# Layer 0's feed-forward down projection with 60 slabs set sooner, four half-depth tiles and eight plain quads, and layer 1's memory keys and values ahead of the keys

## Chip, cores and metric

One core of one Trainium2 chip. The metric is the device time of one execution of the kernel in microseconds (us). Engines: TensorE (PE, the matrix engine; its weight loads are shown apart as PEld), VectorE (DVE), ScalarE (ACT), GpSimd (POOL) and SyncE (SP). SP issues the plain DMAs, POOL those that add while they write.

## What is computed

A two-layer decoder trunk for 256 tokens (T) of width 2048, in float32. Cut to what matters here:

```python
def squared_relu_mlp(h, w1, w2):          # w1 2048x8192, w2 8192x2048
    z = jax.nn.relu(h @ w1)
    return (z * z) @ w2

def reference(x, mem, ...):
    for i in range(2):
        if i == 1:
            sk1, sk2, sv = shared_kv(x, ...)          # rms_norm(x) @ w_kv: keys, then values
        u = rms_norm(x, mix_norm[i]) @ w_in[i]
        ...                                           # i == 0: pooling mixer; i == 1: differential attention
        mem_out = memory_cross_attention(mem_q, mem, mem_norm[i], w_mem_kv[i], ...)
        x = x + concatenate([token_out, mem_out]) @ w_out[i]
        x = x + squared_relu_mlp(rms_norm(x, ffn_norm[i]), w_ff1[i], w_ff2[i])
    return x

def memory_cross_attention(q, mem, mem_norm_g, w_mem_kv, mq_g, mk_g):
    mkv = rms_norm(mem, mem_norm_g) @ w_mem_kv        # its keys and values need only mem, not x
    ...
```

## The kernel before

**Numbers in two parts.** Each float32 operand is split into a high part, rounded to the matrix engine's format, and a low part, the rest. A product is high times high, high times low and low times high, added in PSUM. ScalarE makes the high part (a cast, L177), VectorE the low one (a subtraction, L180).

**Weights.** They lie in memory in the order of use, as blocks of 128 by 128. `Feed` loads them (SP, L141 to L145), splits them and keeps the parts in a ring of six places of 512 columns (`SLOTS`). Four blocks are a quad. `fill` (L226) prepares every quad or slab job three items (`AHEAD`) before its use, and `load` (L125) loads three items more. Plain weights use four raw buffers (`raw`) of 8 blocks.

**A hand-written order.** The program is written as one sequence. `at(d, fn)` puts work `d` ticks later; `tick()` is called once a quad and, where it is written so, once a job. A scheduler at compile time then orders each engine's instructions by this sequence and by its own estimate of when each is ready, so an engine's order may leave the written one.

**Forms of a product.**
- `a_part` (L420): weights stand in the array, 128 outputs wide, and the tokens stream. For a block: one matmul of 512 columns (the high weights by high and low tokens) and one of 256 (the low weights).
- `c_tile` (L443): the same with three matmuls of 256 columns, so that the result needs no addition of two halves.
- `wide_step` (L455): tokens stand in the array, 512 outputs stream; six matmuls of 512 columns for a quad. `b_tile` and `map_tile` run 16 of these over the 16 chunks of the input.

**The feed-forward part, `ffn` (L731), once a layer.** 64 up tiles (`up_tile`, 16 blocks each) make the 64 chunks of z; each goes through a copy (L761), an addition, a ReLU (L824), a square (L832) and a split into z (L772, L776). z holds 16 chunks at a time. The down projection runs between the up tiles by a scheme of seven products in place of eight: a *slab* is two chunks of z (a pair `i`) by 1024 of the 2048 output columns (side `g`: 1 left, 0 right), and its seven products of 128 by 512 go into seven accumulators in PSUM (`banks`). They need sums of z (`combine`, L787, into `sit`, four pairs at a time) and sums of the weights. A slab runs as four jobs (`slab_jobs`, L872) of 6, 3, 6 and 6 matmuls. Its weight sums come from a DMA on POOL's queue that adds to a loaded buffer (`add_right`, L149) and from VectorE's additions (L205, L219). The first job's preparation issues such a DMA for the second, the third one's for the fourth.

There is one set of seven banks for two sides, so every eight slabs a `swap` (L931) copies all banks out and the other side's back. Before, 56 slabs run in each layer: both sides for pairs 0 to 23, then the right side alone for pairs 24 to 31. `tiles_at` (L1034) gives the due time of each slab in up tiles: `p + 8.4` for most, and 1.7 tiles a slab at the end. When the left side ends (pair 23), `close_left` combines its banks, and `turn_left` (L972) transposes it between later up tiles and adds it to the residual.

Twelve jobs are left after up tile 63. `last` (L1097) runs them in pairs between eight `down_tile`s: the left outputs over the remaining chunks 48 to 63 of z, 16 blocks each (`a_part`), with VectorE's additions (L850 to L852). `finish_banks` (L991) closes the right side and transposes it.

**What follows layer 0's feed-forward part.** `done` splits each finished chunk of the residual with its gain into `x_kv`. `later_square` (L710) sums its squares. Then come three key tiles (`map_tile`, 48 quads), three value tiles (48 quads), the memory keys and values of layer 1 (32 quads, input `mems1`), and the queries. `mems1` is made from four reloads of 512 KB of the memory (`mem_again`, L1361), asked for at ticks 46, 55, 64 and 73 into the same four raw buffers as the weights; its 16 chunks are split 6, 8, 10 and 12 ticks after each reload.

## Time and profile before

| | us |
|---|---|
| median of 3 runs | 1997.24 (1997.13 to 1997.51) |
| the profiled execution | 1997.11 |
| its span, first to last instruction | 1995.3 |
| up tiles with slabs, layer 0 | about 268 to 863 |
| the last 12 jobs and 8 down tiles, layer 0 | 863 to 924 |
| key tiles, value tiles | 924 to 991, 991 to 1057 |
| memory keys, memory values | 1057 to 1079, 1079 to 1100 |
| queries and attention, output projection, feed-forward part of layer 1 | 1100 to the end |

How to read the profile: all times are from the start of the span. A row of the timeline is start, duration, engine, line, operation, output and inputs, and count; rows that follow each other closely are merged (`x2`). A duration of a matmul holds its pipelined end, so matmuls overlap, and only the distance between starts tells what one costs. A row of groups is line, engine, operation, output and inputs, shapes and count, then busy time and mean duration in ns, then idle time ahead of them and what ended it. Line numbers are those of the kernel before.

### The profile page before, as it was taken

The numbers are of one execution on the slowest core, as the hardware profiler recorded it, in microseconds if no ns is written. First come the engines' busy times: TensorE is split into PE (matmuls) and PEld (weight loads), VectorE is DVE, ScalarE is ACT, GpSimd is POOL, SyncE is SP. The second block draws the span as 40 slices with busy tenths as digits, with TensorE's granted clock in tenths as the row PEclk, the third lists the DMA queues.
The fourth block names the chain that finished last, engine by engine and source line by source line (L and its number), as shares of the span: only waits on it lengthen the run. The fifth ranks groups of instructions, "written<-read, shape, count | busy, mean of one in ns | idle before, by whom it ended". The sixth has DMA issues, their size and how long they took to land.

```text
span 1995.3 us, 32048 instructions
## 1 busy us (share of the span) xinstructions
PE 1990.6 (100%) x10534; PEld 1704.2 (85%) x10534; DVE 1716.3 (86%) x3089; ACT 1497.9 (75%) x2792; POOL 246.7 (12%) x291
## 2 busy tenths in 40 slices
PE   9999999999999999999999999999999999999999
PEld 8888888888888888888888889888888888888888
DVE  8888878989989899989765698878889898999987
ACT  7765577787887878778665699567787878878775
POOL 0001311111111111110000000311111111111110
PEclk9999999999999999999999999999999999999999
DMA  9556567888888888765566534657888888888775
GB/s 320 174 191 192 189 199 213 225 229 235 227 232 223 226 236 231 220 188 181 189 232 196 172 127 138 200 190 208 228 219 234 230 227 225 227 234 235 218 216 145
DMA packets 142727, 420.10 MB, mean 211 GB/s; under 512 B 16096, under 2 KB 18784, under 8 KB 142560
## 3 DMA queue, kind: packets, MB, share of 16 engines
q1 hardware_dynamic: 110160, 359.32, 55.6%
q0 software_dynamic: 32256, 58.73, 17.4%
q8 instruction: 82, 1.34, 0.3%
q14 instruction: 85, 0.70, 0.1%
q10 hardware_dynamic: 144, 0.01, 0.0%
HBM read 415.90 MB, written 2.10 MB: 209 GB/s over the span
## 4 chain that ended last, share of the span: by engine, by line
PE 100%; DVE 0%; issue 0%
PE x_bank L434 25%; PE x_bank L436 12%; PE p L867 9%; PE p L869 9%; PE p L870 9%; PE wo L434 6%; PE wo L436 3%; PE u L434 2%; PE ff L434 2%; PE u L436 1%; PE q L468 1%; PE k L468 1%; PE q L470 1%; PE q L469 1%; PE k L469 1%; PE v L468 1%
## 5 line engine op out<-in xcount | busy, mean ns | idle before, releaser
L177 ACT CAST hi_ring<-raw 128x512 fp32r<-128x512 f32 x1001 | 613.4, 620 | 270.8 <-PE x_bank L434 69.9
L180 DVE TENSOR_TENSOR lo_ring<-raw,hi_ring 128x512 fp32r<-128x512 f32 x1001 | 687.1, 695 | 121.8 <-ACT hi_ring L177 105.8
L434 PE MATMUL x_bank<-fx,hi_ring 128*128 128x512 f32 x1952 | 610.1, 394 | 0.0
L436 PEld LDWEIGHTS x_bank<-fx,lo_ring 128*128 128x128 f32 x1952 | 366.6, 188 | 83.6
L436 PE MATMUL x_bank<-fx,lo_ring 128*128 128x256 f32 x1952 | 383.5, 278 | 0.0
L434 PEld LDWEIGHTS x_bank<-fx,hi_ring 128*128 128x128 f32 x1952 | 319.8, 189 | 24.1
L177 ACT CAST hi_ring<-room 128x1024 fp32r<-128x1024 f32 x224 | 235.9, 1053 | 128.2 <-PE p L869 107.4
L180 DVE TENSOR_TENSOR lo_ring<-room,hi_ring 128x1024 fp32r<-128x1024 f32 x224 | 274.0, 1223 | 37.6 <-ACT hi_ring L177 29.1
L180 DVE TENSOR_TENSOR lo_ring<-slab,hi_ring 128x512 fp32r<-128x512 f32 (+1 forms) x224 | 213.9, 955 | 60.4 <-ACT hi_ring L177 59.9
L177 ACT CAST hi_ring<-slab 128x512 fp32r<-128x512 f32 (+1 forms) x224 | 185.8, 830 | 40.3 <-PE p L869 23.9
L867 PE MATMUL p<-hi_ring,sit 128*128 128x512 f32 x448 | 175.5, 392 | 0.0
L869 PE MATMUL p<-hi_ring,sit 128*128 128x512 f32 x448 | 175.1, 391 | 0.0
L870 PE MATMUL p<-lo_ring,sit 128*128 128x512 f32 x448 | 174.3, 389 | 0.0
L152 POOL DMA_DIRECT2D room<-in_w x112 | 96.7, 864 | 556.2 <-DVE lo_ring L180 435.3
L152 POOL DMA_DIRECT2D slab<-in_w x112 | 96.9, 865 | 529.1 <-DVE lo_ring L180 513.0
L434 PE MATMUL wo<-cat,hi_ring 128*128 128x512 f32 x512 | 161.7, 397 | 0.0
L867 PE MATMUL p<-hi_ring,z 128*128 128x512 f32 x336 | 132.1, 393 | 0.0
L869 PE MATMUL p<-hi_ring,z 128*128 128x512 f32 x336 | 131.2, 390 | 0.0
L870 PE MATMUL p<-lo_ring,z 128*128 128x512 f32 x336 | 130.8, 389 | 0.0
L436 PEld LDWEIGHTS wo<-cat,lo_ring 128*128 128x128 f32 x512 | 95.9, 188 | 22.3
L436 PE MATMUL wo<-cat,lo_ring 128*128 128x256 f32 x512 | 101.0, 278 | 0.0
L870 PEld LDWEIGHTS p<-lo_ring,sit 128*128 128x128 f32 x448 | 84.1, 188 | 18.6
(373 smaller groups left out, 3372.5 us busy)
## 6 DMA issues: line engine op xcount, KB each, us to landing
raw<-in_w SPq DMA_DIRECT2D x500, 512.0 KB, 4.4
slab<-in_w SPq DMA_DIRECT2D x112, 512.0 KB, 4.7
room<-in_w SPq DMA_DIRECT2D x112, 256.0 KB, 4.7
slab<-in_w POOLq DMA_DIRECT2D x112, 256.0 KB, 6.6
room<-in_w POOLq DMA_DIRECT2D x112, 256.0 KB, 5.8
memraw<-in_mem SPq DMA_DIRECT2D x5, 512.0 KB, 4.4
resid<-in_x SPq DMA_DIRECT2D x8, 256.0 KB, 5.8
out_y<-resid SPq DMA_DIRECT2D x16, 128.0 KB, 1.9
```

The source lines that it names most:

```text
L152: self.nc.gpsimd.dma_start(t, self.wst[h, :, 0:512], accum_op=ALU.add)
L177: self.last_cast = self.nc.scalar.copy(hi, src)
L180: low = self.nc.vector.tensor_sub(lo, src, hi.bitcast(F32))
L434: nc.tensor.matmul(ps, hi, xs[:, k, :], start=first and c == 0, stop=False)
L436: nc.tensor.matmul(ps[:, T : 2 * T], lo, xs[:, k, 0:T], start=False, stop=last and c == len(ks) - 1,)
L468: nc.tensor.matmul(ps[t], x[t][1], hi, start=k == 0, stop=False)
L469: nc.tensor.matmul(ps[t], x[t][0], hi, start=False, stop=False)
L470: nc.tensor.matmul(ps[t], x[t][0], lo, start=False, stop=k == NK - 1)
L867: nc.tensor.matmul(ps, a[1], hi, start=new, stop=False, **again)
L869: nc.tensor.matmul(ps, a[0], hi, start=False, stop=False, **again)
L870: nc.tensor.matmul(ps, a[0], lo, start=False, stop=end, **again)
```

## The change

For layer 0 alone (`full = l == 0`):
- The slabs are 60: after pair 23, the right side for pairs 24 to 27, then the left side for 24 to 27 (with one more swap), then the right side for 28 to 31. The left side closes after pair 27.
- They are due sooner: a new table for the first ones, `p + 7.6` in place of `p + 8.4`, and 0.95 tile a slab at the end. Jobs may all run between the up tiles as far as they are due and their inputs ready.
- `last_full` replaces `last`: all but nine of the jobs left, then half-depth tiles for left outputs 4 to 7 (`c_tile`, chunks 56 to 63 of z only) with three jobs after each of the first three; then eight plain quads (`wide_step`) for left outputs 0 to 3 over the same chunks. The right side is scaled and transposed during these quads, the left side is closed after them (`close`) and transposed during the next stage (`turn_side`). No left transposes run between up tiles.
- `refill` reloads the memory into z's own space during the last jobs, at ticks 1, 5, 10 and 13 after the third half-depth tile, and splits 4 to 7 ticks after each reload.

Then layer 1's memory keys and values run at once, ahead of the key tiles; the squares of the residual are summed during them, and their column form is taken at the key tiles' second tick.

```diff
-    def wide_step(ps, what, xs, k):
+    def wide_step(ps, what, xs, k, ends=(0, NK - 1)):
...
-        slabs += [(0, i, False) for i in range(24, 32)]
+        if full:
+            slabs += [(0, i, True) for i in range(24, 28)]
+            slabs += [(1, i, False) for i in range(24, 28)]
+            slabs += [(1, i, True) for i in range(28, 28)]
+            slabs += [(0, i, False) for i in range(28, 32)]
+        else:
+            slabs += [(0, i, False) for i in range(24, 32)]
+        sooner = (4.5, 6, 8, 9.6, 10.6, 11.5, 12.4, 13.4, 14.4, 15.5, 16.5)
         early = (4.5, 6, 8, 10, 11.2, 12.2, 13.2, 14.2, 15.2, 16.2, 17.4, 18.4)
...
+            if full:
+                if p < 10:
+                    return sooner[p + 1]
+                return p + 7.6 if p <= 50 else 57.6 + 0.95 * (p - 50)
...
-            while len(jobs) > 12:
-                if jobs[0][0] > tiles and (n >= least or not ready(*jobs[0][1:])):
+            while len(jobs) > (0 if full else 12):
+                early_one = jobs[0][0] > tiles
+                if early_one and n >= least or (full or early_one) and not ready(*jobs[0][1:]):
                     break
...
+        def turn_side(side, base, h):
+            t4 = pp.tile([P, 2, T], F32, tag="ot"[h % 2], bufs=1, name="ct")
...
+            c = base + 2 * h
+            nc.vector.tensor_add(resid[:, c : c + 2, :], resid[:, c : c + 2, :], t4)
+            at(1, lambda: done(c))
+            at(2, lambda: done(c + 1))
+
+        def last_full():
+            def some(n):
+                for _ in range(n):
+                    while not ready(*jobs[0][1:]):
+                        tick()
+                    one_job()
+                    tick()
+
+            rest = range(56, 64)
+            some(len(jobs) - 9)
+            for c, t in (("c12", 0), ("v", 1)):
+                scale_rows(left[c], t)
+            for n in range(4, 8):
+                ps = bank()
+                c_tile(ps, "w_ff2", l, n, rest, z)
...
+                at(1, add)
+                if n == 6:
+                    refill(z)
+                if n < 7:
+                    some(3)
+            for d, c, t in ((1, "c11", 0), (2, "c12", 0), (3, "u", 1), (4, "v", 1)):
+                at(d, lambda c=c, t=t: scale_rows(right[c], t))
+            for h in range(4):
+                at((5, 6, 8, 10)[h], lambda h=h: turn_side(right, 8, h))
+            ps = pair_of_banks(0, "ff2")
+            for k in rest:
+                wide_step(ps, ("w_ff2", l, k, 0, 4), z, k % NK, (rest[0] % NK, 63 % NK))
+
+            def close():
+                for t, x in enumerate((left["c11"], left["u"])):
+                    nc.vector.tensor_add(x, x, ps[t])
+                    at(1 + t, lambda x=x, t=t: scale_rows(x, t))
+
+            at(1, close)
+            for e, h in enumerate((2, 3, 0, 1)):
+                at(3 + e, lambda h=h: turn_side(left, 0, h))
...
+    def refill(z):
+        mems_in.append(z)
+
+        def again(p):
+            t = wp.tile([P, 4, T], F32, tag="raw", bufs=RAWS, name="memraw1")
+            nc.sync.dma_start(t, memT[:, 4 * p : 4 * p + 4, :])
+            for k in range(4):
+                at(
+                    4 + k,
+                    lambda k=k: split_gain(z[:, 4 * p + k, :], t[:, k, :], gcol(G_MEM + 16 + 4 * p + k)),
+                )
+
+        for p, d in enumerate((1, 5, 10, 13)):
+            at(d, lambda p=p: again(p))
...
     down()
-    for n in range(NK):
-        at(2 + n // 2, lambda n=n: later_square(n))
+    mems1 = mems_in[0]
+    for i, n in enumerate((8, 9, 10, 11, 12, 13, 14, 15, 0, 1, 2, 3, 4, 5, 6, 7)):
+        at(10 + i, lambda i=i, n=n: later_square(n, i == 0))
+    ps = pair_of_banks(0, "mk1")
+    b_tile(ps, "w_mem_kv", 1, 0, mems1)
+    mrow1 = key_rows(ps, mem_c, P)
+    ps = pair_of_banks(1, "mv1")
+    b_tile(ps, "w_mem_kv", 1, 1, mems1)
...
-    at(12, lambda: c1.extend(columns("x")))
+    at(2, lambda: c1.extend(columns("x")))
     for c in range(3):
         ps = pair_of_banks(c, "k1")
         map_tile(ps, "w_kv", 0, (2 * c, 2 * c + 1, 6 + 2 * c, 7 + 2 * c), x_kv)
```

More of the change, by code (lines that the diff above doesn't have):

```diff
@@ L127, in load @@
             r = self.plan.loads[self.lp]
+            if r[0] == "S" and sum(x[0] == "S" and x[2] == r[2] for x in self.raw) == 3:
+                return
             h = self.plan.row[r]
@@ L960, in close_left @@
                 add(u, u, banks[6])
+            if left is right:
+                return
             for p in of_job[j]:
                 restore(p, 0)
-            if j == 3:
+            if j == 3 and not full:
                 rows = ((left["c11"], 0), (left["c12"], 0), (u, 1), (v, 1))
@@ L1054, in one_job @@
             runs[s](j)
-            if end and s + 1 < len(slabs):
-                if g == 1 and i == 23:
+            if s + 1 == len(slabs):
+                if full:
+                    at(1, lambda: close_left(j, right))
+            elif end:
+                if g == 1 and i == (28 - 1 if full else 23):
                     at(1, lambda: close_left(j))
@@ L1089, in ffn @@
         due(64)
-        assert len(jobs) == 12 and not turns
+        assert full or len(jobs) == 12 and not turns
         feed.loads_ahead = LOADS
```

88 lines of the change are left out of this document (43 added, 45 removed).

## The prediction

> **What bounds the kernel now.** I read the head of the page first, then the chain of waits, then the busy time by stretch, and last the timeline round the end of layer 0's up projection. The columns of the head are busy time, its share of the span, and instructions.
>
> ```profile
> span 1995.3 us, 32048 instructions
> PE 1990.6 (100%) x10534; PEld 1704.2 (85%) x10534; DVE 1716.3 (86%) x3089; ACT 1497.9 (75%) x2792; POOL 246.7 (12%) x291
> PEclk9999999999999999999999999999999999999999
> PE 100%; DVE 0%; issue 0%
> ```
>
> The matrix engine has 4.7 us in which nothing ran, its clock was granted in full throughout, and the chain that ended last stays on it. So an edit pays only through the matrix work it removes, and costs only through a wait that it opens. A busy engine may still be slow, so prices below are taken from start to start, not from the durations, which overlap.
>
> The profiled execution took 1997.11 us, 1.8 us more than its span, and the median of the runs is 1997.24. I sum against 1997.1 and add 0.1 for the median. The next busiest engine decides how much a new wait could cost; here it is by stretch (stretch, its length, then PE, PEld, DVE, ACT, POOL busy with counts, clock, DMA share, GB/s):
>
> ```profile
> 645.00:745.00 100.00, 100.00 (x513) 85.17 (x513) 90.80 (x143) 82.45 (x141) 16.42 (x19) 1.00 0.88 231
> 863.00:924.40 61.40, 61.40 (x340) 53.14 (x339) 57.46 (x105) 46.17 (x84) 3.45 (x4) 1.00 0.60 176
> 924.40:960.00 35.60, 35.60 (x164) 29.59 (x163) 33.47 (x81) 29.44 (x65) 0.00 (x0) 1.00 0.60 187
> 1003.00:1057.00 54.00, 54.00 (x244) 44.81 (x243) 31.55 (x52) 32.50 (x58) 0.00 (x0) 1.00 0.69 229
> 1057.00:1100.00 43.00, 43.00 (x192) 35.59 (x191) 24.34 (x41) 23.11 (x40) 0.00 (x0) 1.00 0.60 192
> 1950.00:1996.00 46.00, 41.61 (x251) 36.74 (x249) 34.02 (x57) 21.88 (x35) 1.73 (x2) 0.99 0.46 136
> ```
>
> Inside the up projection (first row) VectorE is busy for 91%. From the last up tile to the first key step (863 to 924.4) it is 94%, and in the next 36 us 94% again, all without a wait of the matrix engine. The memory keys and values (the row from 1057) load it to 57% only. That is the ground on which the change moves work. (In the last row, 45.3 us to the end of the span, 3.7 us of the idle 4.7 lie behind the last product.)
>
> **The price of a block.** A block is 128 by 128 weights. Four starts give the four prices:
>
> ```profile
> 862.66 0.40 PE L867 MATMUL p<-hi_ring,z 128*128 128x512 f32 x1
> ...
> 864.49 0.39 PE L870 MATMUL p<-lo_ring,sit 128*128 128x512 f32 x1
> ...
> 873.01 0.62 PE L434 MATMUL x_bank<-z,hi_ring 128*128 128x512 f32 x2
> ...
> 877.87 0.63 PE L434 MATMUL x_bank<-z,hi_ring 128*128 128x512 f32 x2
> ```
>
> Eight matmuls of slabs lie between the first two rows: 1.83/8 = 0.229 us each. A slab is 7 products of 3, so 21 x 0.229 = 4.80 us for 16 blocks. Seven pairs of blocks of a down tile lie between the last two: 4.86/7 = 0.694 a pair, 0.347 a block, 5.55 us for 16.
>
> ```profile
> 1985.19 0.28 PE L448 MATMUL ff<-z,hi_ring 128*128 128x256 f32 x1
> ...
> 1987.35 0.28 PE L448 MATMUL ff<-z,hi_ring 128*128 128x256 f32 x1
> ...
> 919.78 0.87 PE ct L1018 x8
> ...
> L470 PE MATMUL mk<-lo_ring,mems x32: 389/389/389, 1057.5 to 1078.6; 128*128 128x512 f32 x32
> ```
>
> The tile with three half-width matmuls a block (c_tile) takes 18 matmuls in 2.16 us: 0.120 each, 0.360 a block. Plain quads: 31 steps of three matmuls in 21.1 us, 0.227 each; six serve 4 blocks, 0.340 a block. Eight transposes: 0.87 us, 0.109 each.
>
> **The change on the matrix engine.** Layer 0's down projection of the left 1024 columns over the last 16 rows of blocks was 8 down tiles of 16 blocks: 128 blocks.
> - 64 of them become four more slabs: 4 x (4.80 - 5.55) = -3.0 us.
> - 32 become the four half-depth tiles: 32 x (0.360 - 0.347) = +0.4. The first matmul of such a tile may start later; I add 0.1.
> - 32 become eight plain quads: 32 x (0.340 - 0.347) = -0.2.
> - Transposes stay 32 (16 for each side), and the moved memory projection keeps its 192 matmuls.
>
> Sum: -2.7 us.
>
> **What is free, and under what cover.** Setting the slabs sooner adds no matmul. Early on (first slabs 0.4 to 0.8 tile sooner) and at the end (a slab each 0.95 tile instead of 1.7) the density is at most slightly over the steady one, a slab a tile, which the 645 to 745 row shows covered at 91% of VectorE. One more exchange of the seven accumulators costs ScalarE 14 copies; it has 17.6 us free in each 100 there. If that cover failed, each late bank would hold a product by about one copy, 0.6 us (row below). The last up tile's result has to reach z sooner, since the first half-depth tile reads it:
>
> ```profile
> 863.16 0.58 ACT L761 COPY room<-x_bank 128x512 f32<-128x512 f32 x1
> 866.91 0.42 DVE L776 TENSOR_TENSOR z<-stage,z 128x256 fp32r<-128x256 f32 x1
> ```
>
> From copy to converted z it takes 867.33 - 863.16 = 4.2 us. Ahead of the tile lie four jobs with 21 matmuls, 4.8 us, and the block in question is its last (2.5 us on). Covered, with about 3 us to spare.
>
> The 16 squares of the residual move from the first key quads to behind quad 10 of the memory projection, whose stretch leaves 18.7 us of 43 on VectorE. Two of the three row buffers are now held through the keys of layer 1; the third is filled once in 16 quads and turned 9 quads later, so it is free in time, and if it were not, the keys would wait some quads of 1.4 us.
>
> **VectorE from the last up tile to the end of the memory keys.** These are its prices (durations; two in a row take 0.60 each, as the last row shows, so about 0.09 of each overlaps):
>
> ```profile
> L180 DVE TENSOR_TENSOR lo_ring<-raw,hi_ring 128x512 fp32r<-128x512 f32 x34 | 22.9, 686 | 2.9 <-ACT hi_ring L177 2.0 <-PE p L869 0.7
> L180 DVE TENSOR_TENSOR lo_ring<-room,hi_ring 128x1024 fp32r<-128x1024 f32 x7 | 8.5, 1220 | 1.2 <-ACT hi_ring L177 1.2
> L330 DVE SCALAR_TENSOR_TENSOR x_kv<-resid,param,x_kv 128x256 fp32r<-128x256 f32 x13 | 5.8, 481 | 0.0
> L851 DVE TENSOR_TENSOR room<-room,r_x 128x256 f32<-128x256 f32 x7 | 2.9, 419 | 0.0
> 870.45 1.28 DVE L180 TENSOR_TENSOR lo_ring<-raw,hi_ring 128x512 fp32r<-128x512 f32 x2
> ```
>
> So 0.60 for 512 columns, 1.13 for 1024, 0.39 for a split with gain, 0.33 for 256 columns. A slab takes 3 x 1.13 + 0.60 + 2 x 0.60 = 5.2 us. In the stretch, where by their due times (63.3 and 64.25 tiles for the slab numbers 56 and 57 of `tiles_at`) 13 jobs are left: 13 jobs (3.25 slabs) 16.9; 32 quads 19.2; four tile additions 2.6; closing right and left sides about 8.4; eight additions of transposes 4.8; 16 splits into x_kv 6.2; 16 splits of the memory 6.2; squares, sums and the last z about 4. Together 68. The matrix engine needs 69 matmuls of jobs (15.8), four half tiles (11.5), 24 quads (32.7) and 32 transposes (3.5): 63.5. VectorE falls behind by about 5 us, most of it during the plain quads. The feed prepares 3 quads ahead, 3 x 1.36 = 4.1 us, so between nothing and 5 us of it shows. I take 0.6, near the bottom, because the stretches of 94% showed none, because only the second bank of the first memory-key quad waits directly for a late addition (the closing of the left side), and because x_kv is not needed until 44 us later.
>
> **The last slab's own chain.** Its third job issues, on POOL's queue, the DMA that adds weights for its fourth. Before, a down tile lay between them; now one job does. The rows (issue by POOL, cast, landing on that queue overall and between 880 and 960):
>
> ```profile
> L152 POOL DMA_DIRECT2D room<-in_w x112 | 96.7, 864 | 556.2 <-DVE lo_ring L180 435.3
> L177 ACT CAST hi_ring<-room 128x1024 fp32r<-128x1024 f32 x224 | 235.9, 1053 | 128.2 <-PE p L869 107.4
> room<-in_w POOLq DMA_DIRECT2D x112, 256.0 KB, 5.8
> room<-in_w POOLq DMA_DIRECT2D x2, 256.0 KB, 4.6
> ```
>
> Third job's cast, subtraction, issue, landing, fourth job's cast and subtraction: 1.05 + 1.22 + 0.86 + 4.6 + 1.05 + 1.22 = 10.0 us. The third job is prepared three items ahead of its use: the job before it (0.7), a half tile (2.9), itself and one job (1.4 each): 6.4 us. So 3.6 us are short. Below stands 0, if the next half tile (2.9 us) and a quad are run ahead of the fourth job. That the compiled order may leave the written one is seen in the chain of waits, where five high parts run before four low ones though they are written two and two:
>
> ```profile
> 175.67 1.25 PE wo L434 x5
> 176.93 0.47 PE wo L436 x4
> ```
>
> I take 0.7. The page "DMA: Bandwidth & Descriptors" of the Trainium skill (section "Anatomy of one DMA — SWDGE (gpsimd) path") puts such a transfer at 2.0 us plus its bytes at 436 GB/s, an estimate of 2.6 us here, by which the shortage would be 1.6; the measured 4.6 decides.
>
> **The sum.** 1997.1 - 2.7 + 0.6 + 0.7 = 1995.7, and 1995.8 with the median's 0.1. Without the waits it is 1994.5; with both at their ends (5 and 3.6), 2003.1.
>
> **Rivals.**
> - *No wait at all.* Both stalls hide: 1994.5. For it: not one long gap in the matrix engine's row before. Against it: 68 us of VectorE work against 63.5.
> - *The matrix engine stands at the fourth job.* The whole shortage and a late VectorE ahead of it (about 1): 1994.5 + 4.6 = 1999.1. The rule that speaks for it is in "TensorE: Matmul & The Clock Gate" of the Trainium skill (section "Step-by-step: what each phase is for"): matmuls stay in program order on the chip, and only weight loads are pulled ahead. So nothing but the compiled order can save it; the two rows above show that order moving, in another stage.
> - *The weight buffers starve, slower than before.* The four reloads of the memory share the four raw buffers of the weights. They were 13 us apart; now they are asked for 4, 5 and 3 quads apart, 4.1 to 6.8 us.
>
> ```profile
> L1363 SPq DMA_DIRECT2D memraw<-in_mem x4: 328/328/328, 985.4 to 1024.4; - x4
> raw<-in_w SPq DMA_DIRECT2D x500, 512.0 KB, 4.4
> ```
>
> With two buffers held, a weight buffer turns over in 4.4 (landing) + 1.4 (second quad) + 0.6 + 0.7 = 7.1 us, one per 3.55, while two quads use one in 2.7. Over some 16 quads that is 8 x 0.85 = 6.8 us, and with VectorE's lead already used nothing absorbs it: 1994.5 + 6.8 + 1.3 = 2002.6. It decides from the point where two are held for longer than the three buffers loaded ahead last, 8 us. Against it: each chunk held its buffer for 12 quads before, over 16 us at a spacing of 13, and those stretches show no wait.
> - *It does more than it says.* Over 4 us gained would need waits that vanish; the 4.7 us of idle in the whole span leave almost none, since 3.7 of them lie at the very end.
>
> **How the numbers follow.** 0.2%, 4.0 us, is about what a measurement of this kernel can tell from no change. Chances: the forecast with a little waiting (1994.9 to 1997.2) 0.48; no wait 0.22; the fourth job's wait, alone or with some of VectorE's (1997.2 to 2001.2) 0.15; starving buffers, or VectorE's whole delay beside the job's, over 2001.2, 0.12; more gain than counted 0.03. So faster by over 0.2% 0.03, slower 0.12, the rest, 0.85, within. The range goes from the sum without waits less 0.4 for rounding in the four prices, 1994.1, to 2001.0, where the starving case begins.
>
> **What would show it.** Four more slabs: 84 more matmuls in the product lines of layer 0, and 60 slabs before the memory keys. Right price: down tiles gone, half-depth tiles at 0.36 a block. VectorE near 100% from the last half tile through the memory keys, and a lighter key stage. Wrong: starts of matmuls more than 0.5 us apart round the last job, or a queue of weight loads waiting for memory splits; then the second or third rival holds. Wrong too: a gap ahead of the first half tile, which would mean that the last z is late.

## The result, and the profile after

The changed kernel takes 2002.57 us (median of 10 runs, 2001.71 to 2003.45), the kernel before 1997.12 (10 runs beside it, 1997.05 to 1997.51): ratio 1.0027, 95% interval 1.0017 to 1.0036. It is slower by 5.45 us, over the bound of 0.2% and above the predicted range, which ended at 2001.0. The profiled execution took 2003.45 us, at the slow end of these runs, with a span of 2001.6.

The head of the page of the changed kernel, and the shares of the chain that ended last:

```profile
span 2001.6 us, 31925 instructions
PE 1992.5 (100%) x10506; PEld 1701.7 (85%) x10506; DVE 1716.2 (86%) x3083; ACT 1502.9 (75%) x2808; POOL 253.4 (13%) x299
PEclk9999999999999999999999999999999999999999
PE 97%; DVE 1%; ACT 1%; DMA 1%; issue 0%; SPq 0%; DVEq 0%; ACTq 0%
```

The clock was granted in full again, so it explains nothing. Before, the chain lay wholly on the matrix engine; now about 3% of it lie on VectorE, ScalarE and DMAs. Those are stretches in which the matrix engine had no lead over what feeds it. They are found by stretch (columns as in the prediction):

```profile
645.00:745.00 100.00, 100.00 (x513) 85.05 (x512) 88.34 (x139) 82.42 (x139) 17.27 (x20) 1.00 0.82 227
880.00:900.00 20.00, 19.03 (x106) 15.60 (x105) 19.96 (x34) 16.14 (x26) 3.45 (x4) 1.00 0.70 166
900.00:920.00 20.00, 19.04 (x110) 16.32 (x109) 18.77 (x33) 12.68 (x23) 0.86 (x1) 1.00 0.56 166
920.00:944.00 24.00, 21.66 (x99) 15.34 (x97) 21.97 (x46) 21.58 (x52) 0.00 (x0) 1.00 0.55 186
944.00:960.00 16.00, 16.00 (x71) 13.25 (x72) 15.31 (x35) 15.86 (x38) 0.00 (x0) 1.00 0.75 258
```

Between 880 and 944 the matrix engine's row is short by 4.3 us. As matmuls overlap, a busy row hides part of a stall, so I also took the distance from each matmul's start to the next, less the pace of its shape (0.227 us for 512 columns, 0.120 or 0.113 for 256, 0.110 for a transpose). From 20 us ahead of the last up tile's end to 130 us behind it that excess is 1.9 us before and 9.8 after. Over the whole execution it is 41.9 and 50.8 (most of the 41.9 is no stall: the up tiles run about 0.008 us a pair over this pace, in both kernels), and what is left of the matrix engine's span, its work at pace, is 1948.7 and 1946.0. **So the change removed about 2.5 us of work** (2.7 by these two figures, 2.5 in the other kernels below) **and opened 9 us of stalls**, 7.8 of them in this stretch; 0.65 lie in the first 100 us, which the change does not touch, and vary from run to run there.

The last up tile ends at 878.1. Behind it lie four groups of stalls, named A to D from here on, with their sizes in excess over the pace. The place is the start of the matmul ahead of the stall. The four make 6.5 us; the rest of the 7.8 is in pieces under 0.12 us.

| stall | where, us | size, us |
|---|---|---|
| A | 884.5, 885.8, 891.8, 898.6 | 0.83, 0.21, 0.42, 0.16 |
| B | 905.4 | 1.13 |
| C | 922.9 to 928.3 | 0.35, 0.17, 0.55, 0.36, 0.21 |
| D | 938.6, 941.0, 943.4 | 0.91, 0.90, 0.30 |

The rows of the timeline round A and B, with the idle time and its releaser in brackets:

```profile
882.75 0.58 ACT L934 COPY p<-room 128x512 f32<-128x512 f32 x1
...
883.58 0.61 ACT L179 CAST hi_ring<-raw 128x512 fp32r<-128x512 f32 x1
...
884.40 1.04 ACT L179 CAST hi_ring<-room 128x1024 fp32r<-128x1024 f32 x1
...
884.92 0.68 DVE L968 TENSOR_TENSOR room<-room,p 128x512 f32<-128x512 f32 x1
...
885.49 0.50 PE L875 MATMUL p<-hi_ring,sit 128*128 128x512 f32 x1 [0.67 <-ACT hi_ring L179]
...
885.52 1.29 DVE L182 TENSOR_TENSOR lo_ring<-raw,hi_ring 128x512 fp32r<-128x512 f32 x2
...
886.26 0.39 PE L452 MATMUL x_bank<-z,lo_ring 128*128 128x256 f32 x1
...
901.80 0.86 POOL L154 DMA_DIRECT2D room<-in_w  x1 [5.08 <-DVE lo_ring L182]
...
906.74 0.50 PE L875 MATMUL p<-hi_ring,z 128*128 128x512 f32 x1 [0.96 <-ACT hi_ring L179]
```

A has two engines in it. Its largest stall (0.83, ended at 885.49) waits for a job's cast on ScalarE, the row at 884.40. ScalarE had no idle time from 880.95 to 887.1, and in its queue ahead of that cast stood, among others, L934, a copy that brings an accumulator of the right side back when the left side closes. The stall of 0.42 (at 891.8) waits for a cast too. The stall of 0.21 (at 885.8, ended at 886.26) waits for the half-depth tile's low part on VectorE (L182 at 885.52), which stands behind L968, one of the operations that close the left side's accumulators. At B the last job waits for its cast, and that cast for the DMA on GpSimd's queue that the job before issued at 901.80. For C and D, the chain of waits and the waits of the engines between 878 and 960 (SP from 890 to 935: total, times, longest) say:

```profile
901.80 3.76 DMA room<-in_w
905.64 1.05 ACT hi_ring L179
...
916.87 5.88 DMA raw<-in_w
```

```profile
PE p L875 <- ACT hi_ring L179: 1.9, 3, 1.0
PE mk L472 <- DVE lo_ring L182: 1.9, 3, 0.7
```

```profile
SPq L143 <- DVE lo_ring L182: 15.3, 6, 4.1
SPq L1432 <- DVE lo_ring L182: 12.2, 3, 5.9
```

C follows a weight load that SP could issue only at 916.87, after its queue had stood for a free raw buffer; L1432, the reload of the memory, takes its turn in the same queue and the same buffers. D is VectorE's order in the memory keys:

```profile
938.20 0.88 DVE L332 SCALAR_TENSOR_TENSOR x_kv<-resid,param,x_kv 128x256 fp32r<-128x256 f32 x2
938.99 0.69 DVE L182 TENSOR_TENSOR lo_ring<-raw,hi_ring 128x512 fp32r<-128x512 f32 x1
939.59 0.48 DVE L332 SCALAR_TENSOR_TENSOR z<-memraw,param,z 128x256 fp32r<-128x256 f32 x1
939.99 0.68 DVE L1150 TENSOR_TENSOR resid<-resid,ct 128x512 f32<-128x512 f32 x1
940.58 0.88 DVE L332 SCALAR_TENSOR_TENSOR x_kv<-resid,param,x_kv 128x256 fp32r<-128x256 f32 x2
941.37 0.69 DVE L182 TENSOR_TENSOR lo_ring<-raw,hi_ring 128x512 fp32r<-128x512 f32 x1
```

From one low part of weights to the next pass 2.4 us, in which two splits into x_kv, one split of the memory and one addition of transposes are done; a memory-key quad needs one low part in 1.36 us.

### The profile page after: what moved, and what is told of

Its sections match the earlier page's. It is cut to its first block, busy times and chain, and to the rows that moved or that the text cites. A ratio compares the mean times of both kernels' runs of the same rounds, so it can differ in the third digit from the quotient of the medians.

```text
span 2001.6 us, 31925 instructions
## 1 busy us (share of the span) xinstructions
PE 1992.5 (100%) x10506; PEld 1701.7 (85%) x10506; DVE 1716.2 (86%) x3083; ACT 1502.9 (75%) x2808; POOL 253.4 (13%) x299
## 3 DMA queue, kind: packets, MB, share of 16 engines
q8 instruction: 82, 1.34, 0.3%
## 4 chain that ended last, share of the span: by engine, by line
PE 97%; DVE 1%; ACT 1%; DMA 1%; issue 0%; SPq 0%; DVEq 0%; ACTq 0%
PE x_bank L436 24%; PE x_bank L438 12%; PE p L875 9%; PE p L877 9%; PE p L878 9%; PE wo L436 6%; PE wo L438 3%; PE u L436 2%; PE ff L436 1%; PE u L438 1%; PE q L470 1%; PE k L470 1%; PE q L472 1%; PE q L471 1%; PE k L472 1%; PE v L470 1%
## 5 line engine op out<-in xcount | busy, mean ns | idle before, releaser
L179 ACT CAST hi_ring<-raw 128x512 fp32r<-128x512 f32 x985 | 600.4, 620 | 256.7 <-DVE lo_ring L182 61.3
L182 DVE TENSOR_TENSOR lo_ring<-raw,hi_ring 128x512 fp32r<-128x512 f32 x985 | 677.5, 697 | 116.9 <-ACT hi_ring L179 102.8
L179 ACT CAST hi_ring<-room 128x1024 fp32r<-128x1024 f32 x232 | 244.3, 1054 | 152.2 <-PE p L877 93.5
L182 DVE TENSOR_TENSOR lo_ring<-room,hi_ring 128x1024 fp32r<-128x1024 f32 x232 | 283.7, 1224 | 61.9 <-ACT hi_ring L179 61.6
L182 DVE TENSOR_TENSOR lo_ring<-slab,hi_ring 128x512 fp32r<-128x512 f32 (+1 forms) x232 | 221.7, 955 | 42.6 <-ACT hi_ring L179 38.2
L875 PE MATMUL p<-hi_ring,sit 128*128 128x512 f32 x464 | 182.0, 392 | 0.9 <-ACT hi_ring L179 0.9
L877 PE MATMUL p<-hi_ring,sit 128*128 128x512 f32 x464 | 181.5, 391 | 0.0
L878 PE MATMUL p<-lo_ring,sit 128*128 128x512 f32 x464 | 180.0, 390 | 0.0
L875 PE MATMUL p<-hi_ring,z 128*128 128x512 f32 x348 | 137.0, 394 | 1.0 <-ACT hi_ring L179 1.0
L877 PE MATMUL p<-hi_ring,z 128*128 128x512 f32 x348 | 136.2, 391 | 0.0
L878 PE MATMUL p<-lo_ring,z 128*128 128x512 f32 x348 | 135.1, 391 | 0.0
```

The costliest lines, as they stand in the source:

```text
L179: self.last_cast = self.nc.scalar.copy(hi, src)
L182: low = self.nc.vector.tensor_sub(lo, src, hi.bitcast(F32))
L875: nc.tensor.matmul(ps, a[1], hi, start=new, stop=False, **again)
L877: nc.tensor.matmul(ps, a[0], hi, start=False, stop=False, **again)
L878: nc.tensor.matmul(ps, a[0], lo, start=False, stop=end, **again)
```

## The experiments

All edits are made to the changed kernel. "Excess" is the sum of stalls in the stretch defined above (9.8 in the changed kernel, 1.9 before). Four small edits return, so they have names: **own buffers** (the memory reloads go to the second buffers of the slabs, which nobody uses by then), **late splits** (x_kv is split 16 ticks later), **last job later** (the last nine jobs stand 3, 3, 2, 1 behind the four half-depth tiles and not 3, 3, 3, 0), **left sooner** (the left side's accumulators close two slabs sooner). The expectations of e1 to e3 letter their theories otherwise than the stalls above: their theory B is the raw buffers (stalls C), their theory C the last slab's DMA (stall B), their theory V VectorE.

| own buffers | late splits | last job later | left sooner | us | excess | run |
|---|---|---|---|---|---|---|
| | | | | 2002.57 | 9.8 | the change |
| x | | | | 2001.55 | 7.9 | e1 |
| | x | | | 1999.61 | 7.0 | e2 |
| | | x | | 2003.41 | 9.4 | e3 |
| | | | x | 2001.51 | 6.9 | e5 |
| x | x | | | 1998.60 | 5.4 | e7 |
| | x | x | | 1998.94 | 6.3 | e8 |
| x | x | x | | 1997.60 | 4.1 | e4 |
| x | x | | x | 1997.62 | 3.9 | e9 |
| x | x | x | x | 1999.04 | 5.1 | e6 |

The excess belongs to the one profiled execution, the time to the median of 6 to 11. The changed kernel's profiled execution is the slowest of its ten, e4's the fastest of its ten, 0.8 us below its median. The runs of one such kernel lie within 0.8 to 2.7 us, so differences under about 0.8 us between these medians decide nothing, and the 1.0 of e1 by itself is hardly more than that.

**e1, own buffers** (its theory B: the raw buffers starve).

```diff
-            t = wp.tile([P, 4, T], F32, tag="raw", bufs=RAWS, name="memraw1")
+            t = feed.second[p % 3].rearrange("p (k t) -> p k t", k=4)
```

> The four reloads of the memory go into the slabs' second buffers, which are free by then, and not into the four raw buffers of the weights; nothing else changes. Theory B (weight loads starve because the reloads hold raw buffers): the gaps of the matrix engine between 920 and 930 us of the changed kernel, about 2.5 us from start to start, go, and the time falls by 2 to 3 us to about 2000. Theory V (VectorE is late): the same splits run at the same place, so the time stays within 0.5 us of 2002.6. Theory C (the last slab's own DMA): no change.

2001.55 us, ratio 1.0022 (1.0013 to 1.0032), 1.0 us less, between its theories B and V. C shrank to one stall of 0.71, D to 1.2, and B stayed at 1.23. The same edit on top of late splits (e2 to e7) also gives 1.0.

**e2, late splits** (theory V: VectorE is late).

```diff
-            at(1, lambda: done(c))
-            at(2, lambda: done(c + 1))
+            at(17, lambda: done(c))
+            at(18, lambda: done(c + 1))
```

> The 16 splits of the residual into x_kv run 16 quads later, in the stretch of the memory values, where VectorE has time; nothing else changes. Theory V: the gaps between 935 and 945 us (2.6 us from start to start) go, and a part of those between 920 and 930, so the time falls by 2.5 to 4 us to about 1999. Theory B: the splits hold no buffer of the weights, so less than 0.5 us is gained. Theory C: no change.

1999.61 us, ratio 1.0012 (1.0003 to 1.0021): the largest single step, 3.0 us. The waits of the matrix engine from 878 to 960 no longer hold VectorE's low parts:

```profile
PE p L875 <- ACT hi_ring L179: 1.8, 3, 0.9
PE mk L470 <- DVE room L1192: 0.7, 1, 0.7
```

D is gone, and of C one stall of 0.81 is left. What it waits for is L1192, the addition that closes the left side, which frees a bank for the memory keys: the one wait for a late addition that the prediction named. It stands on VectorE behind low parts of weights, and those wait for a load that went out at 916.62 and took 6.08 us, as late as in the changed kernel (916.87). So the raw buffers came no sooner. What went out of C is the splits into x_kv, which had stood between those weights' casts and low parts (on ScalarE at 923.37, on VectorE at 924.50). The edit moves both halves of a split, so it relieves ScalarE as well as VectorE. At D the rows above show which of the two was late: VectorE, without a pause from 934.8 on.

**e3, last job later** (its theory C: the last slab's own DMA).

```diff
-                if n < 7:
-                    some(3)
+                some((3, 3, 2, 1)[n - 4])
```

> The very last slab job runs behind the fourth half-depth tile and not ahead of it, which puts 2.9 us of written work between the last slab's third and fourth job. Theory C (its weights' DMA lands too late): the gap at 905 us (1.1 us, 1.3 from start to start) goes, and the time falls by 1 to 1.5 us to about 2001.3. Theories B and V alone: no change, or a little slower, as VectorE's closing of the right side begins 2.9 us later.

2003.41 us, ratio 1.0031 (1.0019 to 1.0043). The stall of 1.13 at the last job is gone, a new one of 0.62 stands 9 us later, waiting for a low part on VectorE, and C and D are as they were. In excess that is 0.4 less, in the median of only six runs 0.8 more. So no time was gained; that the median rose is not explained.

**e4, all three.**

> The three edits together. If the three causes are separate and add up: 6 to 7 us less than the changed kernel, about 1996, with only the gaps between 884 and 893 us (about 2 us) left. If they are one cause seen at three places, the sum is less than the parts: about 1998 to 1999.

1997.60 us, ratio 1.0002 (0.9993 to 1.0012). Alone the three give -1.0, -3.0 and +0.8, together -5.0. Of the stalls over 0.12 us only A is left:

```profile
PE p L875 <- ACT hi_ring L179: 0.9, 2, 0.7
```

```profile
900.00:920.00 20.00, 20.00 (x111) 17.02 (x110) 19.59 (x35) 16.97 (x34) 0.86 (x1) 1.00 0.75 240
920.00:944.00 24.00, 24.00 (x119) 19.89 (x118) 23.22 (x46) 23.77 (x57) 0.00 (x0) 1.00 0.62 204
```

VectorE is busier here (23.22 of 24 us from 920 to 944) than in the changed kernel (21.97), ScalarE too (23.77 against 21.58), and the matrix engine has no idle time. The busy share was no measure of the lateness: what counted was which work stood ahead of the low parts. With A and the small pieces e4 still has 2.2 us more excess than the kernel before, about what the work removed saves, so it only breaks even.

**e5, left sooner** (A is the closing of the left side). Side 0 is the right one in the code and side 1 the left; the expectation muddles the sides in its first sentence, the diff is what ran.

```diff
-            slabs += [(0, i, True) for i in range(24, 28)]
-            slabs += [(1, i, False) for i in range(24, 28)]
-            slabs += [(1, i, True) for i in range(28, 28)]
-            slabs += [(0, i, False) for i in range(28, 32)]
+            slabs += [(0, i, True) for i in range(24, 26)]
+            slabs += [(1, i, False) for i in range(24, 26)]
+            slabs += [(1, i, True) for i in range(26, 28)]
+            slabs += [(0, i, False) for i in range(26, 32)]
```

> Edit: the last slabs in another order: left 24 and 25, right 24 to 27, left 26 to 31 becomes the end of the right side... in short, the left side's accumulators are closed two slabs sooner, so that its closing additions on VectorE (about 8 small ones) no longer fall into the 20 us round the last up tile. The four stalls A (together 1.6 us, 6 to 21 us after the last up tile) are put down to VectorE, which is busy 9.9 to 10.0 of 10 us there. If they come from the closing additions in that place: A shrinks to under 0.6 us, time 2000 to 2001.5 (after: 2002.6), B, C, D as they were (1.1, 1.6 to 2.5, 2.1). If VectorE is simply short of time over the whole stretch, what A loses turns up in C and D: 2002 to 2003. If A is the scheduler's order or the DMA of the third job: A stays at 1.6, 2002 to 2003.

2001.51 us, ratio 1.0021 (1.0012 to 1.0029). A fell from 1.62 to 0.16 us as the first theory had it, so the closing of the left side in that place was its cause. D stayed (2.1), B and C were somewhat smaller in this execution (0.9 and 0.6). But VectorE is as full as it was:

```profile
880.00:900.00 20.00, 20.00 (x120) 17.41 (x120) 20.00 (x33) 15.22 (x24) 3.82 (x5) 1.00 0.74 188
```

It has no idle time in these 20 us, like the 19.96 in the changed kernel, and the matrix engine waits for nothing. So how full VectorE is was not A's cause. The edit takes the closing operations on VectorE (L967 from 883.7 to 862.7) and the copies on ScalarE (the last L934 from 886.0 to 865.1) out of this place together; the rows of A above put the two largest waits to ScalarE, but no run moves one of the two alone.

**e6, all four; e7, own buffers and late splits; e8, late splits and last job later.**

> Edit: the three edits of e4_all_three (own buffers for the memory reloads, the splits into x_kv 16 ticks later, the last job after the last half-depth tile) and the slab order of e5. e4 took 1997.6 with only the stalls A left (1.6 us). If A goes: 1995.8 to 1996.3, 0.05% below before, no more than its matrix work and end allow (prediction's sum without waits was 1994.5). If A stays: 1997 to 1998.

> Edit: own buffers for the reloads and late splits into x_kv together; the last job stays where the change put it. Alone they gave -1.0 and -3.0 us against 2002.6, all three 1997.6. If the waits C and D feed each other (a late raw weight makes VectorE late, a late VectorE holds the raw buffers), the two together give more than 4.0: under 1998.6, and stall B (1.1 us, the last job's weights by POOL's DMA) is all that separates it from 1997.6: 1998.7. If parts simply add: 1998.6 or more, up to 1999.7. If B is absorbed later once nothing behind it is late: 1997.6, the same as all three.

> Edit: late splits into x_kv and the last job after the last half-depth tile; the memory reloads again take the raw weight buffers. What it is slower than e4_all_three (1997.6) is what the raw buffers cost by themselves once VectorE has time and the last job does not wait. If the raw buffers starve the weights whatever VectorE does (the prediction's third rival, 6.8 us over 16 quads): over 2000. If they cost only through VectorE's lateness: 1997.6 to 1998.2. Middle: stall C of about 0.8 to 1.0 stays: 1998.5.

e6: 1999.04 (ratio 1.0008, 0.9999 to 1.0017), a miss: A went, but a stall of 1.34 before a quad and one of 0.81 at a transpose came in its place. e7: 1998.60 (1.0006, 0.9997 to 1.0015), A and B left, B at 1.27: the two parts add (-1.0 and -3.0 make -4.0), so C and D fed each other less than I had thought, and moving the last job is worth 1.0 once they are gone (e7 to e4). With the left side closed sooner the same move costs 1.4 (e9 below to e6). e8: 1998.94 (1.0009, 1.0000 to 1.0018), above its middle case: against e4 the shared raw buffers still cost 1.3 us when VectorE has time. Its larger stall, 1.0 ahead of a plain quad, is not a starved weight:

```profile
913.33 1.71 ACT L414 ACTIVATE z<-memraw,param 128x256 fp32r<-128x256 f32 x4 [1.10 <-DMA memraw<-in_mem]
913.87 0.89 DVE L332 SCALAR_TENSOR_TENSOR z<-memraw,param,z 128x256 fp32r<-128x256 f32 x2 [1.21 <-ACT z L414]
914.67 0.68 DVE L182 TENSOR_TENSOR lo_ring<-raw,hi_ring 128x512 fp32r<-128x512 f32 x1
...
915.41 0.50 PE L472 MATMUL ff<-lo_ring,z 128*128 128x512 f32 x1 [0.84 <-DVE lo_ring L182]
```

The first reload, which had to wait for a raw buffer, was late itself (issued at 908.46, in e4 at 896.00), and the memory's splits stood at the head of ScalarE's and VectorE's queues until it landed, with a weight's low part behind them. The other, 0.6, is again the closing addition behind a late weight load. So of the prediction's third rival a part is real: sharing the buffers costs 1.0 to 1.3 us and not 6.8, and not all of that by starving weights.

**e9, own buffers, late splits, left sooner.**

> Edit: e7's two edits (own buffers for the reloads, splits into x_kv 16 ticks later) and e5's slab order (the left side's accumulators closed two slabs sooner, so that its additions on VectorE leave the 20 us round the last up tile); the last job stays where the change put it. So A, C and D are treated and B alone is left. If the stalls are told apart rightly: B alone, 0.9 to 1.3 us, 1996.8 to 1997.4. If closing the left side sooner only brings the jobs forward to meet the DMA on POOL's queue sooner (as the two stalls of 1.34 and 0.81 in e6 suggest), B grows to 1.5 to 2.5 and the time stays at 1998 to 1999.

1997.62 us (1.0002, 0.9993 to 1.0010), between the two expectations: A, C and D are gone and 1.15 us near the last job are left in three pieces.

**e10, the memory's low parts on GpSimd.**

```diff
+    def split_gain_pool(dst, src, g):
+        nc.scalar.activation(dst[:, 0:T], src, AF.Copy, scale=g)
+        x = vt("scaled")
+        nc.gpsimd.tensor_scalar_mul(x, src, g)
+        nc.gpsimd.tensor_sub(dst[:, T : 2 * T], x, dst[:, 0:T].bitcast(F32))
...
-                    lambda k=k: split_gain(z[:, 4 * p + k, :], ...),
+                    lambda k=k: split_gain_pool(z[:, 4 * p + k, :], ...),
```

> Edit: against the changed kernel, the low part of the 16 splits of the memory goes from VectorE (one operation, 0.48 us) to GpSimd (a multiplication into an own tile and a subtraction), which gives VectorE 7.6 us back between the last half-depth tile and the middle of the memory keys; buffers, x_kv, jobs and slabs as in the change. If D is VectorE's lateness: D (2.1 us) goes, 1999.6 to 2000.5, as with e2, which took 7.3 us of other work out of the same stretch. If D is the place of the splits into x_kv in VectorE's queue rather than its load: D stays, 2002 to 2003. If GpSimd is too slow, the first memory key quads wait for z's low part: a new gap at 'mk' behind GpSimd, 2003 to 2006.

2006.07 us (1.0043, 1.0029 to 1.0057), the third case. The groups on GpSimd between 890 and 960 (busy, mean ns):

```profile
L420 POOL TENSOR_SCALAR scaled<-memraw,param 128x256 f32<-128x256 f32 x16 | 20.7, 1304 | 10.8 <-PE x_bank L457 6.9 <-DMA memraw<-in_mem 3.9
L421 POOL TENSOR_TENSOR z<-scaled,z 128x256 fp32r<-128x256 f32 x16 | 15.7, 999 | 0.0
```

GpSimd needs 2.3 us where VectorE needs 0.48, and a memory-key quad stands 4.3 us while GpSimd still splits. With the matrix engine that late, that D is absent tells nothing.

**e11, jobs 4, 3, 1, 1 in e6; e12, the same and e10's edit.**

```diff
-                some((3, 3, 2, 1)[n - 4])
+                some((4, 3, 1, 1)[n - 4])
```

> Edit: e6's four, but the last nine jobs stand 4, 3, 1, 1 behind the four half-depth tiles instead of 3, 3, 2, 1, so that a half-depth tile (2.9 us) stands between the third and the fourth job of both last slabs. In e6 the fourth jobs, right behind the third, waited 0.36 and 1.34 and a transpose 0.81 us. If the DMA that the third job issues for the fourth is the cause: those two go, 1996.3 to 1997.3. If VectorE is late whatever the order: 1998.5 to 1999.5.

> Edit: e11 and the memory's low parts on GpSimd (as in e10). Nothing of the known stalls is left if each was named rightly: under 1 us of stalls, 1995.0 to 1996.3, where the prediction's sum without waits was 1994.5 and its forecast 1995.8. If the rest of e11 is not VectorE's: the same as e11.

e11: 1999.21 (1.0011, 1.0002 to 1.0020), no gain over e6. The stall in front of the last jobs is now 1.59, and ScalarE's waits between 878 and 910 show another way to it:

```profile
ACT z L414 <- DMA room<-in_mem: 1.6, 1, 1.6
```

A high part of the memory stood at the head of ScalarE's queue until its reload landed at 899.80, and a job's cast stood behind it. e12: 2015.58 (1.0091, 1.0078 to 1.0105): GpSimd again, a stall of 12.2 us at the memory keys; a miss by 20 us, from which nothing follows for the rest.

**e13, e9 with the last job behind the second plain quad; e14, e11 with the memory's splits two ticks later; e15, e13 with that too.** In e13 the loop over the plain quads calls `some(1)` behind its second, with the scaling and turning of the right side put after it; e14's edit is one number:

```diff
-                    4 + k,
+                    6 + k,
```

> Edit: e9 (own reload buffers, late splits into x_kv, left side closed two slabs sooner) with one job more moved: the last job stands behind the second of the eight plain quads and not ahead of them, so that the DMA that its predecessor issues has a half-depth tile and two quads (5.6 us) for its 3.8 us of landing and the cast behind it. If that DMA is all of B: the stalls of e9 at 24.8 to 26.9 us (1.15 together) go, 1996.3 to 1996.7. If they move, as they did with e3 and e6, because something else is late by then: 1997.3 to 1998.5.

> Edit: e11 with the memory's splits 6 to 9 ticks behind their reload instead of 4 to 7. In e11 a high part of the memory stood 1.60 us at the head of ScalarE's queue for its reload, the cast of a job's weights behind it, and the matrix engine 1.4 us for that cast. If that is e11's stall: it goes, and 1999.2 becomes 1997.3 to 1998.0. If the weights' own DMA would have been as late: 1999, no change.

> Edit: e13 and e14's later splits of the memory. If each of the waits that are left was named rightly, nothing above 0.3 us is left in the stretch: 1995.4 to 1996.3, beside 1997.3 before, which is what the matrix work removed (2.7 predicted, about 2.4 seen) leaves after rounding. If the removed work does not show even then, the price of a block was wrong: 1997.

All three missed: 1997.84 (1.0003, 0.9994 to 1.0011), 1999.14 (1.0010, 1.0001 to 1.0019), 1998.02 (1.0003, 0.9994 to 1.0012). In e13 the stall moved from the job to the fourth half-depth tile (1.42): it waited for L1173, the multiplication that reads an earlier such tile out of PSUM, which stood on VectorE behind low parts, and those behind casts, and these behind the cast that waited for a DMA on GpSimd's queue and behind high parts of the memory.

```profile
899.67 1.05 ACT L179 CAST hi_ring<-room 128x1024 fp32r<-128x1024 f32 x1 [2.53 <-DMA room<-in_w]
...
900.75 1.23 DVE L182 TENSOR_TENSOR lo_ring<-room,hi_ring 128x1024 fp32r<-128x1024 f32 x1 [1.22 <-ACT hi_ring L179]
...
904.60 0.41 DVE L1173 TENSOR_TENSOR room<-x_bank,r_x 128x256 f32<-128x256 f32 x1
```

In e14 ScalarE waited for the reload in the same place as in e11 (1.7 us): two ticks in the written sequence left its compiled order round that wait as it was, so the run tested nothing.

**e16, e17, e18: e9, e13 and e11 with the first two reloads asked for at ticks 4 and 7 instead of 1 and 5.**

```diff
-        for p, d in enumerate((1, 5, 10, 13)):
+        for p, d in enumerate((4, 7, 10, 13)):
```

> Edit: e9 with the first two reloads of the memory issued 4 and 7 ticks behind the third half-depth tile instead of 1 and 5. In e9 the DMA on GpSimd's queue that begins 0.6 us ahead of the first reload lands after 5.5 us, the next after 3.8. If the reload's traffic slows it: about 3.8, the cast behind it 1.7 us sooner, e9's stalls of 1.15 us at 24.8 to 26.9 us under 0.4, 1996.4 to 1997.0. If it is slow by itself: still 5.5, and 1997.6. If the memory is then late for the memory keys: a stall at 'mk', 1998 to 2000.

> Edit: the same in e13 (last job behind the second plain quad). In e13 the fourth half-depth tile waited 1.2 us for an addition on VectorE (L1173) that stood behind low parts waiting for the cast of that slow DMA's weights. If that chain is right: the stall of 1.42 goes to under 0.4, 1996.3 to 1996.9. If the addition is late for another reason: 1997.8 as e13.

> Edit: the same in e11 (jobs 4, 3, 1, 1). In e11 a high part of the memory waited 1.6 us on ScalarE for the reload, with a weight cast behind it; e14's later ticks left it in its place. With the reload itself moved by three jobs, its high parts move behind that cast in ScalarE's order: if that wait is e11's stall (1.59), it goes and 1999.2 becomes 1997.0 to 1998.0. If not: 1999.

1997.81 (1.0002, 0.9993 to 1.0011), 1997.94 (1.0002, 0.9993 to 1.0011), 1999.60 (1.0010, 1.0001 to 1.0018), and the same stalls. The edit did not reach the queue: SP issued the first reload at 894.59 in e16 and 894.85 in e9. What the runs do show is the DMA on GpSimd's queue with and without the reload beside it. Its issues between 893 and 897, KB and us to landing, first in e5, then in e9, then in e4:

```profile
room<-in_w POOLq DMA_DIRECT2D x1, 256.0 KB, 3.6
```

```profile
room<-in_mem SPq DMA_DIRECT2D x1, 512.0 KB, 5.1
room<-in_w POOLq DMA_DIRECT2D x1, 256.0 KB, 5.5
```

```profile
room<-in_mem SPq DMA_DIRECT2D x1, 512.0 KB, 4.4
room<-in_w POOLq DMA_DIRECT2D x1, 256.0 KB, 4.0
```

e5 has e9's slabs and jobs, but its reload comes at 903.6. In e9 the reload is issued 0.6 us behind this DMA, and so it is in e6, e13 and e15 to e17, where the DMA landed after 5.5 to 5.9 us. In e4 (and e1 and e7) it is issued 0.9 us behind, and the DMA landed after 3.9 to 4.0. So a reload beside it is not enough to make it slow, and no edit moved the reload alone. There is a second suspect. ScalarE's rows in e9, and the wait of the matrix engine there:

```profile
899.80 1.05 ACT L179 CAST hi_ring<-room 128x1024 fp32r<-128x1024 f32 x1 [2.56 <-DMA room<-in_w]
...
901.23 1.71 ACT L414 ACTIVATE z<-room,param 128x256 fp32r<-128x256 f32 x4
902.84 1.65 ACT L179 CAST hi_ring<-raw 128x512 fp32r<-128x512 f32 x3
```

```profile
PE ff L470 <- ACT hi_ring L179: 0.5, 1, 0.5
```

The quad that waits needs the last of the three casts at 902.84. Ahead of them stand the slow DMA's cast and also four high parts of the memory, 1.71 us, which the early reload set free. Later high parts alone would have told the two apart; e14 and e15 tried that, but in both ScalarE's order stayed. So the 1.2 us or so that are left of B come from that DMA, from the memory's high parts, or from both; this stays open.

No run beat the kernel before: the best, e4, e9, e16 and e17, stand at 1.0002 of it, which is no difference.

## Why the prediction was wrong

- **The matrix work was right.** -2.7 us was predicted. The work at pace fell from 1948.7 to 1946.0 here and to 1946.2 in the other kernels, by 2.7 and 2.5. The slabs' product lines gained the 84 matmuls: 448 x 3 + 336 x 3 before, and now 464 x 3 + 348 x 3:

```profile
L875 PE MATMUL p<-hi_ring,sit 128*128 128x512 f32 x464 | 182.0, 392 | 0.9 <-ACT hi_ring L179 0.9
L875 PE MATMUL p<-hi_ring,z 128*128 128x512 f32 x348 | 137.0, 394 | 1.0 <-ACT hi_ring L179 1.0
```

- **Most of the edits put at nothing cost nothing.** From 645 to 745 VectorE is at 88% and the matrix engine at 100%; from 100 to 858 us no start is late by 0.25 us. The squares behind quad 10 opened no gap from 944 on, and the first half-depth tile began without a gap, so the last z was there in time. (One line of the change, in `load`, which stops loading ahead while three slab buffers of a kind are filled, is not in the list of the change; no run tests it alone.) The exception is ScalarE. Its copies for the exchange were taken as covered by the 17.6 us that it has free in each 100. Where the left side now closes it had none free from 880.95 to 887.1, and 1.25 of A's 1.62 us are waits for its casts.
- **The step that failed is "VectorE falls behind by about 5 us ... so between nothing and 5 us of it shows. I take 0.6, near the bottom".** What showed of VectorE is D, 2.1 us, and part of C, and e2, which moved 16 splits out of the way, gave 3.0 us. Three reasons were given for the bottom. "The stretches of 94% showed none" does not carry over: e4 shows none at 97%, the change 2.3 us of idle matrix engine at 92%. "Only the second bank waits for a late addition" named a real wait, which shows in e1, e2 and e8 at 0.6 to 0.8 us; but in the change what was late were the weights' own low parts, behind other work in VectorE's queue. And "x_kv is not needed until 44 us later" was true, but the splits stood ahead of low parts that were needed at once.
- **The stretch was summed as one.** 68 us of VectorE against 63.5 with a lead of 4.1 says little about when the lead runs out. From 880 to 900 VectorE has no idle time in e5 either, and nothing waits; from 938 to 943 two splits, an addition and a split stand between one low part and the next, and each quad waits. ScalarE was not summed over this stretch at all. Also, 14 jobs and not 13 were left behind the last up tile.
- **The last slab's own chain: mechanism right, size near it partly by luck.** 0.7 taken, 1.13 seen. From the third job's cast (899.58) to the end of the fourth's (906.69) the chain took 7.1 us and not 10.0. The sum counted the issue's 0.86 us twice, since landing is timed from the start of the issue (901.80 and 3.76 us above); it ended with a subtraction of 1.22 us for which the first matmul does not wait; and the landing took 3.76 and not 4.6. Against that, the compiled order ran only five matmuls, 0.9 us, of the last half-depth tile and the plain quads ahead of the last job, not a half tile and a quad. That a DMA of this kind can take 5.5 us here, and that the memory's high parts get ahead of weight casts (e9), was not in it.
- **The shared buffers came in small.** As third rival they had 6.8 us and in the forecast nothing; e1, and e8 against e4, price them at 1.0 and 1.3. The forecast's argument against them, that each chunk once held its buffer over 16 us without a wait, came from a stage where nothing else held raw buffers late. That this rival's time, 2002.6, is the measured one is chance: it has a wait of 6.8 us that did not occur and leaves A and most of D out.
- **The waits were treated as chances apart.** 1994.5 without waits was close: 1997.1 less the 2.5 gives 1994.6. But A, B, C and D all came in one execution.

## What to carry to other kernels

A denser schedule is paid for by the engines that prepare operands: check each one's queue for what stands ahead of the next operand, item by item, at the densest 20 us, and not its busy share over 100. Work that is needed late (here 16 splits with 44 us to spare) should also be written late when the same queue feeds the matrix engine. And stalls close together are not independent: removing one may gain nothing, as in e3, gain a microsecond once others are gone (e7 to e4), or cost more than that beside yet another (e9 to e6). So try edits together before dropping or keeping one.

## What the runs showed of the hardware beyond that

- A DMA on GpSimd's queue that adds 256 KB of weights landed in 3.6 to 3.7 us with no 512 KB load issued within 2.8 us of it (e2, e3, e5, e8), in 5.5 to 5.9 us with a 512 KB load issued 0.6 us behind it (e6, e9, e13, e15 to e17), and in 3.9 to 4.0 us with that load 0.9 us behind (e1, e4, e7). With a 512 KB load issued 1.4 us ahead of it, near 884, it took anything from 4.5 to 6.5 us (e5, e6, e9, e11 to e18). What decides is open.
- The same low part costs 0.48 us in one operation on VectorE and 1.30 + 1.00 us in two on GpSimd (e10).
